# Group 0's first product in another order: M2, M1, M3, M6, M7, M5, M4 in a Winograd-tiled squared-ReLU MLP

## Chip, cores and metric

One core of one Trainium2 chip. The metric is the device time of one execution in microseconds; before the change the median of three runs is 1235.79 us (1234.95 to 1236.64).

## The reference, cut to what matters

One layer of a hybrid encoder over 1024 tokens plus 16 meta tokens, width 1024, all in float32: an input projection, stick-breaking attention, a Conformer convolution and a short gated convolution, an output projection, and then the part that the change touches:

```python
h = layer_norm(ALPHA * h + mix, ln_mix_g, ln_mix_b)
ff = jnp.square(jax.nn.relu(h @ w1)) @ w2      # w1: 1024 x 4096, w2: 4096 x 1024
h = layer_norm(ALPHA * h + ff, ln_ff_g, ln_ff_b)
return h[:, 16:]
```

## The kernel before

**Number format.** Every float32 matmul operand is split into a high part (ScalarE, L128) and a low part (VectorE, L129, the source minus the high part). A product is three passes: high x high, high x low, low x high. `split_turned` (L802) does the same with the sign turned (L807, L808).

**The MLP by groups.** The 4096 hidden columns are taken in eight groups of 512. Per group a first product (`first_product`, L915: hidden rows from h and w1, then squared ReLU) and a second product (in `group`, L1056: hidden rows times w2, added into `acc`). Both are done by Winograd's form of Strassen's scheme on 2 x 2 blocks: seven block products in place of eight, at the price of block sums and differences on VectorE. `acc` holds the normalised stream, [128 rows of a tile, 8 tiles, 1024 columns]; `order` is (6, 7, 4, 5, 0, 1, 2, 3), the order in which the output projection finishes row tiles.

**The seven operands from h.** In the first product the operands xb21, xb11 (blocks of h), xt2, xt3, xt4, xt1 (sums and differences) and xb22 are [128, 2 (high, low), 4, 512] tiles, each filled by four `x1_block` calls (L796): four transposes into one PSUM tile (tag t, three buffers; L799), then a split. For group 0 this is done while the projection ends: two x1_block calls for xb21 and xb11 per row tile (`x1_first`, L816), and for the last tiles `x1_t2` (L821): difference d3 = right half minus left half, d2 = d3 plus the other tile's left half, and the transposed, turned split into xt2. Operands that later groups use again stay in SBUF (xt1, xt2, xt4); xb21, xb11, xt3 and xb22 are written to DRAM (xscr 0 to 3, on SP's queue) and loaded again in each later group.

**Group 0 before.** M2 = early[0] x xb21 into a new pair of banks, kept as c11 (`keep_sum`, L898: two ScalarE copies). M1 = early[1] x xb11 into pair pa; c11 = relu2(c11 + pa) (`relu2`, L902: an add on VectorE, L906, ReLU and square on ScalarE, L907 and L908). Weight sums a11 += a21, part b, a11 += a22, part a; the last two x1_t2 and the blocks of xt3 (`second_half`, L1126). M6 = a x xt2 on top of pa, kept as c21. M7 = b x xt3 into pair pb, kept as c22. Then xt3 is written out and xt4 and xt1 are built (`third_half`, L1135). M4 = a22 x xt4 on top of pb, giving c21; M5 = a21 x xt1 on top of pa, giving c22; a12 += a11, xb22 is built (`last_block`, L1149), and M3 = a12 x xb22 on top of pa gives c12 straight from PSUM. `part` (L862) is a split into one of five ring buffers. The generator's yields let `group` put its own work between: the sums of the w2 blocks at the first, and at the second (before M3) the difference a21 = c22 - c21 and the splits that open the second product.

**After it.** `end_transposes` (L1158) releases the PSUM pool of the first phase, and the second product's banks come from a new pool over the same eight banks. The first matmul of the second half follows.

**What sets the order.** Program order gives each instruction its priority, and the compiler's scheduler simulates all engines and issues on each, in order, what its own model finds ready. On the chip each engine works through that fixed list. SP's queue carries the loads and stores, POOL's queue the accumulating load `w2_add` (L998).

Of the kernel before, what the change touches and what calls it, by code (L numbers as in the profile page):

```python
# [8 lines left out]
F32 = mybir.dt.float32  # L9
# [27 lines left out]
def f32(ap):  # L37
    return ap.bitcast(F32)
# [3 lines left out]
def hybrid_layer(ctx: ExitStack, tc, x, meta_tokens, ln_in_g, ln_in_b, w_in, w_conf_dw, b_conf_dw,  # L42
# [747 lines left out]
    def x_tile(pl, tag, dt=F32R):  # L790
        return pl.tile([P, 2, 4, 512], dt, tag=tag, bufs=1, name=f"x_{tag}")

    xb21, xb11, xt2 = [x_tile(x1p, tag) for tag in ("X", "Y", "T2")]
    diffs = x_tile(x1p, "T1", F32)

    def x1_block(hl, src, cols, turned=False):  # L796
        pt = ps_t([P, 4, P])
        for k in range(4):
            nc.tensor.transpose(out=pt[:, k], in_=src[:, k * P:(k + 1) * P], identity=ident)  # L799
        split_turned(hl[:, 0, :, cols], hl[:, 1, :, cols], pt, turned)  # L800
# [9 lines left out]
    def vsum(dst, a, b, op):  # L810
        nc.vector.tensor_tensor(out=dst, in0=a, in1=b, op=op)  # L811

    def cols_of(t):
        return slice(t % 4 * P, (t % 4 + 1) * P)
# [3 lines left out]
        x1_block(xb21, acc[:, t, HALF[1]], cols_of(t))  # L818
        x1_block(xb11, acc[:, t, HALF[0]], cols_of(t))

    def x1_t2(t):  # L821
        x, y = acc[:, t], acc[:, 4 + t]
        vsum(diffs[:, 0, t], x[:, HALF[1]], x[:, HALF[0]], ALU.subtract)
        vsum(diffs[:, 1, t], diffs[:, 0, t], y[:, HALF[0]], ALU.add)
        x1_block(xt2, diffs[:, 1, t], cols_of(t), True)

    done = 0
    for i in range(FIRST, 8):
        run(mix_tiles(i, i + 1))
        while done < min(4 + i - FIRST, 2 * (i - FIRST + 1)):  # L830
            if done < 4:
                x1_first(done)
            else:
                x1_t2(order[done])
            done += 1
    x = acc[:, order[7], :]
    ln_rows_dve(x, x, P, lnq[order[7]], *norm)
# [1 line left out]
        nc.sync.dma_start(out=xscr[i], in_=f32(x))  # L839
    attw.release()  # L840
    x1q = pool("x1q", side="right")
    xt4 = x_tile(x1q, "T4")

    def w1_block(k, c0):

# [16 lines left out]
    def part(src, k, turned=False):  # L862

        hl = ring("hl").rearrange("p s (k c) -> p s k c", k=k)
        split_turned(hl[:, 0], hl[:, 1], src, turned)
        return hl
# [35 lines left out]
    def relu2(r, pr, sign, more=True):  # L902

        for j, bk in pieces2(pr):
            if more:
                nc.vector.tensor_tensor(out=r[:, j], in0=bk, in1=r[:, j], op=ALU.add)  # L906
            nc.scalar.activation(out=r[:, j], in_=r[:, j] if more else bk, func=AF.Relu, scale=sign)  # L907
            nc.scalar.activation(out=r[:, j], in_=r[:, j], func=AF.Square)  # L908
# [6 lines left out]
    def first_product(g):  # L915

        r0, r1 = (wA.tile([P, 2, S], F32, tag="ff", bufs=2, name="relu2") for _ in range(2))
        c11, c12, c21, c22 = (r[:, :, h] for r in (r0, r1) for h in HALF)
        if g == 0:
            pc = pair(0)  # L920
            product1(early[0], xb21, pc, True)
            keep_sum(c11, pc)
            pa = pair(0)
            product1(early[1], xb11, pa, True)
            a11, a21, a12, a22 = w1_load(0)
            relu2(c11, pa, 1.0)
            vsum(a11, a11, a21, ALU.add)
            b = part(a11, 4)
            vsum(a11, a11, a22, ALU.add)
            a = part(a11, 4)  # L930
            xt3 = second_half()
            yield
            product1(a, xt2, pa, False)
            keep_sum(c21, pa)
            vsum(a21, a21, a22, ALU.add)
            pb = pair(0)
            product1(b, xt3, pb, True)
            keep_sum(c22, pb)
            xt1 = third_half(xt3)
            a = part(a22, 4)  # L940
            product1(a, xt4, pb, False)
            relu2(c21, pb, -1.0)
            a = part(a21, 4)
            product1(a, xt1, pa, False)
            relu2(c22, pa, -1.0)
            vsum(a12, a12, a11, ALU.add)
            x = last_block()
            xres.append(xt1)
        else:
            a11, a21, a12, a22 = w1_load(g)  # L950
            xt1 = xres[0]
            x = load_x("X", 0)
            a = part(a11, 4)
            pa = pair(g)
            product1(a, x, pa, True)
            keep_sum(c11, pa)
            vsum(a11, a11, a21, ALU.add)
            x = load_x("Y", 2)
            a = part(a11, 4)
            pb = pair(g)  # L960
            product1(a, x, pb, True)
            keep_sum(c22, pb)
            vsum(a11, a11, a22, ALU.add)
            a = part(a11, 4)
            yield
            product1(a, xt2, pa, False)
            keep_sum(c21, pa)
            a = part(a22, 4)
            product1(a, xt4, pb, False)
            relu2(c21, pb, -1.0)  # L970
            vsum(a21, a21, a22, ALU.add)
            a = part(a21, 4)
            product1(a, xt1, pa, False)
            relu2(c22, pa, -1.0)
            x = load_x("X", 1)
            a = part(a12, 4)
            pc = pair(g)
            product1(a, x, pc, True)
            relu2(c11, pc, 1.0)
            vsum(a12, a12, a11, ALU.add)  # L980
            x = load_x("Y", 3)
        a = part(a12, 4)
        yield r0, r1
        product1(a, x, pa, False)
        relu2(c12, pa, 1.0, False)
# [70 lines left out]
    def group(g):  # L1056
# [11 lines left out]
        t3, t2, t4 = b22, b12, b21  # L1068
        r0, r1 = next(steps)
        a11, a21, a12, a22 = (r[:, :, HALF[1 - th]] for r in (r1, r0) for th in range(2))  # L1070
        vsum(a21, a11, a21, ALU.subtract)
        b, a = part(b11, 2), part(a11, 2)
        w2_add(b11, g, 0, 1)
        b_, a_ = part(t3, 2), part(a21, 2)
        for _ in steps:
            pass
        if first:
            end_transposes()
        vsum(a21, a21, a22, ALU.add)
        pa = [bank2() for _ in range(2)]  # L1080
        product(a, b, pa, True)
# [41 lines left out]
        split(hl[:, 0], hl[:, 1], raw)  # L1123
        return hl

    def second_half():  # L1126

        x1_t2(order[6])
        x1_t2(order[7])
        xt3 = x_tile(x1p, "X")  # L1130
        for t in range(4):
            x1_block(xt3, diffs[:, 0, t], cols_of(t))
        return xt3

    def third_half(xt3):  # L1135

        nc.sync.dma_start(out=xscr[2], in_=f32(xt3))
        for t in range(4):
            d = diffs[:, 1, t]
            vsum(d, d, acc[:, 4 + t, HALF[1]], ALU.subtract)  # L1140
            x1_block(xt4, d, cols_of(t))
        xt1 = x_tile(x1p, "T1")
        for t in range(4):
            d = cst.tile([P, 512], F32, tag="sq", bufs=1, name="d1")
            vsum(d, acc[:, 4 + t, HALF[0]], acc[:, t, HALF[0]], ALU.subtract)
            x1_block(xt1, d, cols_of(t))
        return xt1

    def last_block():  # L1149
        xb22 = x_tile(x1p, "Y")  # L1150
        for t in range(4):
            x1_block(xb22, acc[:, t, HALF[1]], cols_of(t))
        nc.sync.dma_start(out=xscr[3], in_=f32(xb22))
        return xb22

    ps2 = None

    def end_transposes():  # L1158
# [42 lines left out]
```

## Time and profile before

| | |
|---|---|
| median of three runs | 1235.79 us |
| the profiled execution | 1235.24 us, span of the trace 1233.3 us |
| PE busy | 1151.8 us, 93% |
| DVE busy | 975.3 us, 79% |
| ACT busy | 561.8 us, 46% |
| POOL busy | 97.7 us, 8% |
| mean granted TensorE clock | 0.973 of full speed |

Times in the trace are microseconds from the start of the span. A row of a timeline gives start, length, engine, line, operation and tiles; in square brackets stands the idle time before it and what ended that. Names lose their numbers and can be those of an earlier tile in the same memory: `d3` and `d2` appear as x_T, w1's blocks as w_raw, c11 to c22 as relu. Matmuls overlap, so the length of a row holds the tail of its last one.

### The profile page before, as it was taken

How to read it: one execution, taken by the hardware profiler on the slowest of the kernel's cores; microseconds unless marked ns; L12 is line 12 of the kernel's file. 1: busy time of each engine (PE TensorE's matmuls, PEld its weight loads, DVE VectorE, ACT ScalarE, POOL GpSimd, SP SyncE). 2: the span in 40 equal slices, each digit the busy share in tenths (PEclk: the TensorE clock that was granted, in tenths of full speed). 3: DMA queues.
4: the chain of work that ended last, by engine and by line, in shares of the span. 5: the costliest groups of instructions: out<-in, count | busy, mean ns of one | idle time of the engine just before them, and what ended most of it. 6: DMA issues, size and time to landing. Idle time of an engine off the chain costs nothing.

```text
span 1233.3 us, 15574 instructions
## 1 busy us (share of the span) xinstructions
PE 1151.8 (93%) x5982; PEld 990.3 (80%) x5982; DVE 975.3 (79%) x1203; ACT 561.8 (46%) x951; POOL 97.7 (8%) x219
## 2 busy tenths in 40 slices
PE   5999997889989798998989999999999999999994
PEld 5999996779889677886768888888888888888883
DVE  6799976978878789968968688596885958859588
ACT  4522114656657556434553353433535345352444
POOL 3300002010010000034000000000000000000003
PEclk9999998899999899998999999999999999999998
DMA  9304211020021442112773653736537265372427
GB/s 293 129 20 101 69 52 51 18 52 19 18 52 35 117 141 69 53 34 85 251 258 140 221 205 108 270 116 222 209 122 278 90 222 222 134 273 72 154 69 204
DMA packets 63753, 161.80 MB, mean 131 GB/s; under 512 B 3337, under 2 KB 27184, under 8 KB 59584
## 3 DMA queue, kind: packets, MB, share of 16 engines
q1 hardware_dynamic: 56704, 144.52, 32.8%
q0 software_dynamic: 5056, 10.49, 4.6%
q10 hardware_dynamic: 1920, 5.81, 1.2%
q8 instruction: 47, 0.77, 0.3%
q14 instruction: 26, 0.21, 0.0%
HBM read 135.63 MB, written 18.87 MB: 125 GB/s over the span
## 4 chain that ended last, share of the span: by engine, by line
PE 66%; DVE 9%; ACT 4%; issue 2%; POOL 1%; DMA 1%; DVEq 0%; ACTq 0%
PE ps_g L885 24%; PE ps_g L894 24%; PE ps_g L210 6%; PE ps_g L630 5%; DVE keepp L463 2%; PE ps_t L513 2%; PE ps_g L455 2%; PE ps_o L486 1%; PE ps_o L489 1%; DVE beta L465 1%; DVE al L129 1%; ACT keepp L459 1%; DMA q_hl<-q_hl 1%; DVE acc L122 1%; ACT ah L128 0%
## 5 line engine op out<-in xcount | busy, mean ns | idle before, releaser
L894 PE MATMUL ps_g<-hl 128*128 128x512 f32 x1344 | 307.4, 390 | 2.9 <-DVE hl L129 1.6
L894 PEld LDWEIGHTS ps_g<-hl 128*128 128x128 f32 x1344 | 251.8, 188 | 57.4 <-DVE hl L129 2.0
L210 PE MATMUL ps_g<-xh,w_hl 128*128 128x346 f32 (+4 forms) x1024 | 259.8, 333 | 0.9 <-ACT beta L460 0.9
L210 PEld LDWEIGHTS ps_g<-xh,w_hl 128*128 128x128 f32 x1024 | 180.6, 192 | 10.0 <-ACT beta L460 1.1
L210 PE MATMUL ps_g<-xl,w_hl 128*128 128x346 f32 (+4 forms) x512 | 170.3, 333 | 0.7 <-DVE xl L129 0.7
L1010 DVE TENSOR_TENSOR acc<-acc,ps_g 128x1024 f32<-128x1024 f32 x96 | 116.0, 1215 | 23.2 <-PE ps_g L894 23.2
L885 PE MATMUL ps_g<-x_T,hl 128*128 128x512 f32 x576 | 133.4, 390 | 0.8 <-DVE hl L129 0.4
L885 PEld LDWEIGHTS ps_g<-x_T,hl 128*128 128x128 f32 x576 | 107.6, 188 | 24.3 <-DVE hl L129 0.8
L210 PEld LDWEIGHTS ps_g<-xl,w_hl 128*128 128x128 f32 x512 | 98.5, 192 | 5.0 <-DVE xl L129 1.0
L128 ACT CAST hl<-relu 128x1024 fp32r<-128x1024 f32 x48 | 50.6, 1054 | 106.6 <-PE ps_g L894 106.3
L463 DVE TENSOR_TENSOR_SCAN keepp<-keepp 128x912 f32<-128x912 f32 (+7 forms) x64 | 87.7, 1380 | 10.2 <-ACT keepp L459 9.6
L885 PE MATMUL ps_g<-x_Y,hl 128*128 128x512 f32 x384 | 90.5, 390 | 2.0 <-ACT x_Y L128 1.2
L885 PEld LDWEIGHTS ps_g<-x_Y,hl 128*128 128x128 f32 x384 | 71.8, 188 | 17.8 <-ACT x_Y L128 1.5
L885 PE MATMUL ps_g<-x_X,hl 128*128 128x512 f32 x360 | 84.3, 389 | 1.3 <-DVE x_X L129 1.3
L128 ACT CAST hl<-w_raw 128x1024 fp32r<-128x1024 f32 x55 | 55.4, 1049 | 62.5 <-DVE w_raw L811 62.5
L285 DVE SCALAR_TENSOR_TENSOR cacc<-glu,prm,cacc 128x482 f32<-128x482 f32 (+3 forms) x120 | 82.7, 745 | 0.3
L129 DVE TENSOR_TENSOR hl<-w_raw,hl 128x1024 fp32r<-128x1024 f32 x55 | 65.2, 1220 | 20.5 <-ACT hl L128 20.5
L885 PEld LDWEIGHTS ps_g<-x_X,hl 128*128 128x128 f32 x360 | 67.5, 188 | 15.5 <-DVE x_X L129 1.6
L906 DVE TENSOR_TENSOR relu<-ps_g,relu 128x1024 f32<-128x1024 f32 (+1 forms) x27 | 29.8, 1104 | 51.4 <-PE ps_g L885 51.4
L630 PE MATMUL ps_g<-w_hl,y 128*128 128x512 f32 x240 | 65.2, 409 | 1.8 <-DVE w_hl L129 1.7
L459 ACT ACTIVATE keepp<-ps_g 128x456 f32<-128x456 f32 (+8 forms) x112 | 51.8, 467 | 32.7 <-PE ps_g L455 14.9
L455 PE MATMUL ps_g<-ks,q_hl 128*128 128x456 f32 (+8 forms) x224 | 58.1, 362 | 8.3 <-ACT beta L460 3.9
(209 smaller groups left out, 1752.5 us busy)
## 6 DMA issues: line engine op xcount, KB each, us to landing
x_X<-xscr SPq DMA_DIRECT2D x14, 2048.0 KB, 7.7
x_Y<-xscr SPq DMA_DIRECT2D x14, 2048.0 KB, 8.4
w_raw<-in_w_ff_dram SPq DMA_DIRECT2D x16, 1024.0 KB, 8.8
w<-in_w_ff_dram SPq DMA_DIRECT2D x32, 512.0 KB, 6.5
raw<-in_w_in_dram SPq DMA_DIRECT2D x22, 512.0 KB, 4.2
b<-in_w_ff_dram SPq DMA_DIRECT2D x16, 512.0 KB, 3.6
xt<-in_x_dram SPq DMA_DIRECT2D x8, 512.0 KB, 5.2
h_scr<-ht ACTq DMA_DIRECT2D x8, 512.0 KB, 3.2
```

The source lines that it names most:

```text
L128: nc.scalar.copy(out=h, in_=src)
L129: nc.vector.tensor_tensor(out=l, in0=src, in1=f32(h), op=ALU.subtract)
L210: nc.tensor.matmul(dst[:, :cw], lhsT=w[:, a, k, :], rhs=b[:, k, c0:c0 + cw], start=(i == 0), stop=(i == 3 * KT - 1))
L285: nc.vector.scalar_tensor_tensor(out=acc, in0=glu[j][:, o + k:o + k + n], scalar=prm[:, j, k:k + 1], in1=acc, op0=ALU.mult, op1=ALU.add)
L455: nc.tensor.matmul(zp[:, :cm], lhsT=qs[h][:, m, i * P:(i + 1) * P], rhs=ks[:, h, c0:c0 + cm], start=(m == 0), stop=(m == 1 and not last))
L459: nc.scalar.activation(out=kp[h][:, c0:c0 + cw], in_=zp[:, :cw], func=AF.Sigmoid, scale=-0.125)
L463: nc.vector.tensor_tensor_scan(out=rev, data0=rev, data1=rev, initial=1.0, op0=ALU.mult, op1=ALU.bypass)
L630: nc.tensor.matmul(dst, lhsT=y[a][:, t * P:(t + 1) * P], rhs=w[b][:, n * 512:(n + 1) * 512], start=(i == 0), stop=(i == last))
L885: nc.tensor.matmul(bk, lhsT=a[:, u, k, j * P:(j + 1) * P], rhs=x[:, v, k, :], start=(start and i == 0), stop=(i == 11), skip_group_check=True)
L894: nc.tensor.matmul(prs[tt // 2][:, tt % 2], lhsT=a[:, x, u, tt * P:(tt + 1) * P], rhs=b[:, y, u, :], start=(start and i == 0), stop=(i == ...
L906: nc.vector.tensor_tensor(out=r[:, j], in0=bk, in1=r[:, j], op=ALU.add)
L1010: nc.vector.tensor_tensor(out=a, in0=a, in1=prs[h], op=op)
```

## The change

In group 0 alone the seven products come in another order: M2, M1, M3, M6, M7, M5, M4 (before: M2, M1, M6, M7, M4, M5, M3). xb22 gets a buffer of its own at once (tag Y; xb11 moves to tag T4), and the blocks of xb22 take the places that x1_t2 had among the last projection tiles. M3 goes into a pair of banks of its own and is kept as c12. The differences d3 and d2 live in two ring buffers and are made after M3, d3 being used again for xt1's differences and d2 for xt4's. M5's sum in pa then serves c22 and c12, both with an add. The last product is M4, giving c21. In `group` the splits of b11 and c22 come before the last product of group 0, and the difference a21 = c22 - c21 behind it. Later groups change only in which of xt1 and xt4 comes by `xres`.

```diff
-    xb21, xb11, xt2 = [x_tile(x1p, tag) for tag in ("X", "Y", "T2")]
-    diffs = x_tile(x1p, "T1", F32)
+    xb21, xb11, xt2, xb22 = [x_tile(x1p, tag) for tag in ("X", "T4", "T2", "Y")]
...
-    def x1_t2(t):
+    def x1_b22(t):
+        x1_block(xb22, acc[:, t, HALF[1]], cols_of(t))
+
+    def x1_t2(t, d3, d2):
         x, y = acc[:, t], acc[:, 4 + t]
-        vsum(diffs[:, 0, t], x[:, HALF[1]], x[:, HALF[0]], ALU.subtract)
-        vsum(diffs[:, 1, t], diffs[:, 0, t], y[:, HALF[0]], ALU.add)
-        x1_block(xt2, diffs[:, 1, t], cols_of(t), True)
+        vsum(d3, x[:, HALF[1]], x[:, HALF[0]], ALU.subtract)
+        vsum(d2, d3, y[:, HALF[0]], ALU.add)
+        x1_block(xt2, d2, cols_of(t), True)
...
-                x1_t2(order[done])
+                x1_b22(order[done])
...
-    xt4 = x_tile(x1q, "T4")
+    xt1 = x_tile(x1q, "T1")
...
             product1(early[1], xb11, pa, True)
             a11, a21, a12, a22 = w1_load(0)
             relu2(c11, pa, 1.0)
+            for t in order[6:]:
+                x1_b22(t)
             vsum(a11, a11, a21, ALU.add)
             b = part(a11, 4)
             vsum(a11, a11, a22, ALU.add)
+            vsum(a12, a12, a11, ALU.add)
+            a = part(a12, 4)
+            pb = pair(0)
+            product1(a, xb22, pb, True)
+            keep_sum(c12, pb)
+            d3, d2 = (f32(ring("diffs")).rearrange("p s (t c) -> p (s t) c", t=2) for _ in range(2))
+            for t in order[4:]:
+                x1_t2(t, d3[:, t], d2[:, t])
             a = part(a11, 4)
-            xt3 = second_half()
-            yield
             product1(a, xt2, pa, False)
             keep_sum(c21, pa)
-            vsum(a21, a21, a22, ALU.add)
+            nc.sync.dma_start(out=xscr[3], in_=f32(xb22))
+            xt3 = x_tile(x1p, "X")
+            for t in range(4):
+                x1_block(xt3, d3[:, t], cols_of(t))
             pb = pair(0)
             product1(b, xt3, pb, True)
             keep_sum(c22, pb)
-            xt1 = third_half(xt3)
+            nc.sync.dma_start(out=xscr[2], in_=f32(xt3))
+            yield
+            vsum(a21, a21, a22, ALU.add)
+            for t in range(4):
+                vsum(d3[:, t], acc[:, 4 + t, HALF[0]], acc[:, t, HALF[0]], ALU.subtract)
+                x1_block(xt1, d3[:, t], cols_of(t))
+            a = part(a21, 4)
+            product1(a, xt1, pa, False)
+            for r, sign in ((c22, -1.0), (c12, 1.0)):
+                relu2(r, pa, sign)
+            xt4 = x_tile(x1p, "T4")
+            for t in range(4):
+                vsum(d2[:, t], d2[:, t], acc[:, 4 + t, HALF[1]], ALU.subtract)
+                x1_block(xt4, d2[:, t], cols_of(t))
+            xres.append(xt4)
             a = part(a22, 4)
+            yield r0, r1
             product1(a, xt4, pb, False)
             relu2(c21, pb, -1.0)
-            a = part(a21, 4)
-            product1(a, xt1, pa, False)
-            relu2(c22, pa, -1.0)
-            vsum(a12, a12, a11, ALU.add)
-            x = last_block()
-            xres.append(xt1)
+            return
...
-        vsum(a21, a11, a21, ALU.subtract)
         b, a = part(b11, 2), part(a11, 2)
         w2_add(b11, g, 0, 1)
+        if first:
+            run(steps)
+            end_transposes()
+        vsum(a21, a11, a21, ALU.subtract)
         b_, a_ = part(t3, 2), part(a21, 2)
-        for _ in steps:
-            pass
-        if first:
-            end_transposes()
+        run(steps)
```

`second_half`, `third_half` and `last_block` are removed; what they did stands in the lines above.

## Rows read from the trace of the kernel before

**Rows 1.** The page's busy time, share of the span and instructions, by engine.

```profile
PE   1151.8 (93%) x5982; PEld 990.3 (80%) x5982; DVE 975.3 (79%) x1203; ACT 561.8 (46%) x951; POOL 97.7 (8%) x219
```

**Rows 2.** The chain that ended last: start, us, what.

```profile
643.75 38.37 PE ps_g L894 x168
...
1177.16 27.21 PE ps_g L894 x120
```

**Rows 3.** Windows: us, busy time by engine (instructions), PE clock, DMA share, GB/s.

```profile
573.60:616.00 42.40, 33.49 (x151) 25.80 (x150) 40.87 (x54) 23.01 (x40) 5.11 (x11) 0.84 0.63 225
616.00:643.75 27.75, 24.43 (x121) 18.68 (x119) 16.89 (x23) 15.33 (x26) 0.28 (x1) 1.00 0.72 259
...
587.70:643.75 56.05, 50.29 (x241) 39.39 (x239) 43.65 (x56) 31.47 (x51) 1.28 (x1) 0.97 0.75 263
643.75:1210.00 566.25, 564.65 (x2489) 467.08 (x2490) 427.39 (x385) 241.67 (x243) 10.97 (x12) 1.00 0.48 172
...
580.00:585.00 5.00, 3.47 (x13) 2.12 (x11) 5.00 (x6) 2.25 (x5) 1.16 (x3) 0.50 0.00 0
585.00:590.00 5.00, 4.18 (x14) 3.31 (x15) 5.00 (x8) 1.19 (x2) 0.00 (x0) 0.50 0.50 210
590.00:595.00 5.00, 5.00 (x24) 4.13 (x23) 3.58 (x7) 1.99 (x3) 0.00 (x0) 0.90 0.99 418
```

**Rows 4.** Timeline of PE, 587 to 645 us: M2 and the rows with waits.

```profile
587.71 6.81 PE L885 MATMUL ps_g<-x_X,w_slot 128*128 128x512 f32 x22
...
597.47 4.83 PE L885 MATMUL ps_g<-x_Y,hl 128*128 128x512 f32 x20 [0.72 <-DVE hl L129]
...
605.00 4.83 PE L885 MATMUL ps_g<-x_T,hl 128*128 128x512 f32 x20 [0.41 <-DVE hl L129]
...
612.47 5.29 PE L885 MATMUL ps_g<-x_X,hl 128*128 128x512 f32 x22 [1.31 <-DVE x_X L129]
...
619.42 0.73 PE L885 MATMUL ps_g<-x_T,hl 128*128 128x512 f32 x2 [0.34 <-ACT x_T L128]
...
627.52 0.66 PE L799 MATMUL ps_t<-ident,d 128*128 128x128 f32 x4 [0.94 <-DVE d L811]
...
637.04 6.02 PE L885 MATMUL ps_g<-x_Y,hl 128*128 128x512 f32 x24 [1.24 <-ACT x_Y L128]
643.75 26.59 PE L894 MATMUL ps_g<-hl 128*128 128x512 f32 x116 [0.69 <-ACT relu L907]
```

**Rows 5.** Timeline of DVE, 573 to 587 us, in front of M2.

```profile
573.67 0.69 DVE L811 TENSOR_TENSOR x_T<-acc 128x512 f32<-128x512 f32 x1
574.27 0.68 DVE L129 TENSOR_TENSOR x_X<-ps_t,x_X 128x512 fp32r<-128x512 f32 x1
...
585.06 1.22 DVE L811 TENSOR_TENSOR w_raw<-w_raw 128x1024 f32<-128x1024 f32 x1
586.20 0.69 DVE L129 TENSOR_TENSOR x_X<-ps_t,x_X 128x512 fp32r<-128x512 f32 x1
```

**Rows 6.** Timeline of ACT at the end of M2.

```profile
592.03 0.59 ACT L900 COPY relu<-ps_g 128x512 f32<-128x512 f32 x1 [3.34 <-PE ps_g L885]
592.51 1.05 ACT L128 CAST hl<-w_raw 128x1024 fp32r<-128x1024 f32 x1
```

**Rows 7.** Timelines of DVE and ACT at the end of the first half.

```profile
634.96 0.69 DVE L906 TENSOR_TENSOR relu<-ps_g,relu 128x512 f32<-128x512 f32 x1 [1.81 <-PE ps_g L885]
...
636.88 0.64 ACT L908 ACTIVATE relu<-relu 128x512 f32<-128x512 f32 x1
...
637.63 1.21 DVE L811 TENSOR_TENSOR relu<-relu 128x1024 f32<-128x1024 f32 x1
...
641.03 1.22 DVE L129 TENSOR_TENSOR hl<-relu,hl 128x1024 fp32r<-128x1024 f32 x1
```

**Rows 8.** Timeline of SP's queue: group 1's load of x_Y.

```profile
644.71 0.32 SPq L912 DMA_DIRECT2D x_Y<-xscr  x1
```

**Rows 9.** DMA issues, 560 to 650 us: engine, count, KB each, us to landing.

```profile
b<-in_w_ff_dram POOLq DMA_DIRECT2D x1, 512.0 KB, 11.4
```

More of the change, by code (lines that the diff above doesn't have):

```diff
@@ L938, in first_product @@
             keep_sum(c22, pb)
-            xt1 = third_half(xt3)
+            nc.sync.dma_start(out=xscr[2], in_=f32(xt3))
[13 more added lines that the diff above has]
+            xres.append(xt4)
             a = part(a22, 4)
+            yield r0, r1
             product1(a, xt4, pb, False)
             relu2(c21, pb, -1.0)
-            a = part(a21, 4)
-            product1(a, xt1, pa, False)
-            relu2(c22, pa, -1.0)
-            vsum(a12, a12, a11, ALU.add)
-            x = last_block()
-            xres.append(xt1)
+            return
         else:
             a11, a21, a12, a22 = w1_load(g)
-            xt1 = xres[0]
+            xt4 = xres[0]
             x = load_x("X", 0)
@@ L1124, in early_part @@
         return hl
[L1126 to L1154, printed above, removed]
     ps2 = None
```

## The prediction

> **What bounds the kernel now.** I read the busy shares first, then the chain that ended last, then the windows, then the timelines of single engines. The busy shares put PE at 93% and DVE at 79% of the span [rows 1]: an average that says where the room is not. The chain places it: from 643.75 us on it is unbroken PE work, one 38 us piece per half group, to the last group [rows 2], and the windows say the same (564.65 us busy of 566.25) [rows 3]. So whatever brings forward the first matmul of group 0's second half, at 643.75, brings the whole rest forward by as much; nothing later can swallow it, and nothing later can give more.
>
> The stretch before, from the last projection matmul at 573.60 to 643.75, is where PE waits. It falls in two. Up to 616.0 DVE is busy 40.87 of 42.40 us; from there to 643.75 only 16.89 of 27.75 [rows 3]. The front is DVE's, the rear is PE's with holes. From the start of M2's main run at 587.71, PE is busy 50.29 of 56.05 us [rows 3]. The holes have names in PE's timeline: 0.72 at M1 (its weights' low half), 0.41 at M6 (the same), 1.31 at M7 (a block of x_X), 0.34 at M4 (a block of x_T), 0.94 at a transpose (a difference d), 1.24 at M3 (a block of x_Y), and 0.69 at the very end, where the second half waits for the last read of the first half's PSUM [rows 4]. The first six sum to 4.96 us.
>
> **The change, part by part.** The seven products, the 28 blocks of transposes and the sixteen half-row differences all stay; their order changes.
>
> *Two more adds and copies.* M3 becomes a product of its own, so c12 is kept (two ScalarE copies, 0.59 each [rows 6]) and added later (two DVE adds of 0.69 [rows 7]); its two ReLUs read SBUF instead of PSUM. On DVE, half-row operations start 0.60 apart and full ones 1.14 [rows 5]; two adds cost 1.2 us of DVE's time. They follow M5, while PE runs M4; in the rear DVE has 10.9 us free [rows 3]. On the path: 0. If DVE were full there, 1.2.
>
> *Start of M2.* DVE runs without a gap from 573.60 to M2 and the last x_X low half goes at 586.20 [rows 5]. In front of it stand four differences for T2 (573.67 is one); they move behind M3 and release 4 x 0.60 = 2.4 us. In their place come at most two low halves of B22 blocks, 1.2 us, which may also go after M2's operand. A weight sum at 585.06 stands in front of the last x_X too [rows 5]; if it is the one for M5, moved behind M7 in the code, it may give another 1.14. Ends: 0 (the gaps are filled by other ready work) and 3.6 us. I take **1.8 us**, half the sum of the ends and between 1.2 and 2.4, what the counted operations give by themselves.
>
> The granted clock was 0.50 from 580 to 590, after PE had idled, and came back during 590 to 595, where PE was busy the whole 5 us (mean 0.90) [rows 3]; M2's 22 matmuls took 6.81 us against 5.29 for the 22 of M7 [rows 4], a loss of 1.5 us. I let this loss move with M2 unchanged. The Trainium skill (TensorE: Matmul & The Clock Gate, Part 1 on the clock gate) says that it is PE's own activity that lifts the throttle, not time since some event. By that, the loss stays 1.5 us and the sum below holds; were the return fixed at about 591 us, M2 starting 1.8 us earlier would win about 0.9 us less.
>
> *The six holes.* Before, M6 follows M1 in the same bank and M4 follows M7 in the same bank, each behind a read of that bank. Now every product that accumulates has another between: M3 between M1 and M6, M5 between M7 and M4. B22's blocks need only finished rows, so M3's 1.24 us wait on x_Y has no cause left. Does DVE deliver each operand in time? From M2 at 585.9 (1.8 us earlier), with 5.5 us a product, 0.5 a block (38.37 us for 168 matmuls [rows 2]; the blocks are my estimate from the 0.66 us that one block takes alone in the 627.52 row [rows 4], less overlap):
> - M3 is due at 585.9 + 6.8 + 1 + 5.5 = 599.2. DVE owes before it the last rows' norm, an x_Y half, four B22 halves, M1's low half, three weight sums and two low halves: 7 x 1.14 + 5 x 0.60 = 11, so 596.9.
> - M6 is due at 599.2 + 5.5 + 2 = 606.7. DVE owes two adds, eight differences, four T2 halves, one low half: 14 x 0.60 + 1.14 = 9.5, so 606.4. This is the tight one.
> - M7: 2.4 us of DVE, ready at 608.8, due at 614.2.
> - M5: three W2 sums, one weight sum, one low half and eight half operations, 10.5, so 619.3 against 621.7.
> - M4: 4.8 + 1.14 + 1.14 (b11's low half), so 626.4 against 629.2.
>
> PE's due times are strict here: by them M4 would end at 634.7, 3 us before what the old timeline gives once 1.8 and 3.5 us are taken off (638.4 for the second half's start), since they hold no cost of switching between transposes and products.
>
> The order on DVE and ScalarE is fixed by a scheduler's own estimate, not by these due times (M1's cast stands behind c11's copy, which waits 3.34 us, on ScalarE [rows 6]), so some of the holes will reappear: I let 1.5 of the 4.96 come back. Gain **3.5 us**; ends 0 and 5.0.
>
> *The end.* What ends the first half changes from c12 to c21, and c21 feeds the second product of the second half. Chain behind M4's last matmul: add 0.69, ReLU and square 0.64 each, difference 1.21, cast 1.05, low half 1.22 [rows 6, 7], 5.4 us plus hand-overs, some 5.8. Its cover is the first product of the second half (c22 and b11, both ready), which starts about 0.7 after M4, as before, and lasts 5.5: 6.2. Hidden by 0.4 if nothing stands before it on DVE. The next sum on a21, another full operation, and the cast and low half for the third product also slip behind M4. I charge **0.5 us**; ends 0 and 2.5 (two full DVE operations in the way).
>
> *DMAs and queues.* On SP, xscr[3] is written before xscr[2] instead of 25 us after it, and both before M5; group 1's loads of x_X and x_Y wait for these writes and for M7 and M3, all earlier now (x_Y's load went at 644.71 [rows 8], needed by 682). Group 1's W1 loads wait for the parts of a21 and a22, which move later by about 10 us, but are needed only after 38 us of PE work. POOL's accumulating load of b11 (11.4 us to land [rows 9]) is next read some 22 us after the second half begins. Cost 0; if that cover went, group 1 would open with a hole of a few us. Ring buffers: the two differences take two of five, and each later part finds one freed by a finished product: 0.
>
> **Sum:** 1.8 + 3.5 - 0.5 = 4.8 us less. The profiled execution took 1235.24, 0.55 below the median of 1235.79; off the median that is **1231.0 us**. The ends: 3.6 + 5.0 = 8.6 less, 1227.2; and 2.5 more, 1238.3.
>
> **Rivals.** 0.2%, 2.5 us, is about what a measurement of this kernel can tell from no change.
> - *DVE takes the holes back.* For it: up to 616 DVE is nearly full, M6 is met within 0.3 us above, and the change adds 1.2 us to DVE. Then waits at M1, M3, M6 and M5 replace the old ones, M2 gains 1.2 and the holes about 0.5: 1.7 - 0.5 = 1.2 less, 1234.6. Against: 10.9 us of idle DVE behind 616 that moved work can use. Chance 0.22, a fifth of it still faster than 1233.3.
> - *The order does not take.* The scheduler may issue M3 late or the differences early all the same, as it now runs differences ahead of x_X halves [rows 5]. About 1235. Chance 0.06, since each engine still has to serve M3 first in the code.
> - *Slower: c21's chain lies open.* If the first product of the second half is held as well (c22's part queued behind the adds on DVE), or stands behind c21's part, PE idles through the whole 5.8 us and the two or three full operations behind it for the third product, some 8 us in all. It decides once the wait at the second half's opening passes 5.3 + 2.5 = 7.8 us. Time: 1235.8 - 5.3 + 8 = 1238.5. For it: that add, two activations, a difference and a split all follow the last product, where before only a ReLU did. Both DVE and ScalarE serve their queues strictly in order, as the Trainium skill says too (TensorE: Matmul & The Clock Gate, "Architectural detail", on queue depths), and ScalarE's 3.34 us wait in front of a ready cast [rows 6] agrees. Against: c22 is finished one product ahead. Chance 0.10.
>
> **How the numbers follow.** The forecast (gain of 2.5 to 8.6 us) has 0.62; with the fifth of the first rival, faster is 0.66; the rest of it and the second make 0.24 for the same; slower is 0.10. A range from 1227.0 to 1236.5 leaves out the slower rival and a little of the far ends.
>
> **What would show it.** In the changed trace: M3 as third product with no wait on x_Y; M2's main run near 586; holes between M2 and M4 of 1 to 2 us in sum instead of 4.96; the wait in front of the second half still about 0.7, and its second product's wait under 1; that half's start near 638.4; unbroken PE after it. It is wrong if M2 has not moved (the DVE term), if waits on hl or on differences of 4 us or more stand before M6 and M5 (the holes), or if the first two products of the second half wait several us on a part of relu (the end).

## The result, and the profile after

The changed kernel takes 1242.72 us (median of 6 runs, 1240.89 to 1244.47) against 1235.86 for the kernel before on the same chip (6 runs, 1234.95 to 1236.64): ratio 1.0061, 95% interval 1.0049 to 1.0073, 6.9 us slower. The prediction was 1231.0, in the range 1227.0 to 1236.5. The profiled execution took 1242.26 us, span 1240.3, mean clock 0.972. One execution below, of run 8's ten, took 1458.1 us at a mean clock of 0.748 and is left out of that run's ratio.

The page's busy shares hardly differ from [rows 1]: DVE has the 1.1 us that two more adds cost, PE 3.8 us more for the same 5982 matmuls.

```profile
PE 1155.6 (93%) x5982; PEld 993.4 (80%) x5982; DVE 976.4 (79%) x1205; ACT 563.4 (45%) x953; POOL 96.6 (8%) x219
```

So the difference is in waiting and in slow PE time, and the timeline of PE places it. Its columns: start, duration, engine, line, operation, tiles, shape, count, and in brackets the idle time in front and what ended it.

```profile
584.47 1.97 PE L798 MATMUL ps_t<-ident,acc 128*128 128x128 f32 x8 [0.52 <-DVE x_T L129]
586.09 5.71 PE L887 MATMUL ps_g<-x_X,w_slot 128*128 128x512 f32 x22
...
592.43 5.73 PE L887 MATMUL ps_g<-x_T,hl 128*128 128x512 f32 x24
599.87 1.20 PE L887 MATMUL ps_g<-x_Y,hl 128*128 128x512 f32 x4 [1.71 <-ACT hl L128]
602.88 6.45 PE L887 MATMUL ps_g<-x_Y,hl 128*128 128x512 f32 x20 [1.81 <-DVE hl L129]
609.18 1.47 PE L798 MATMUL ps_t<-ident,diffs 128*128 128x128 f32 x12
613.60 2.44 PE L798 MATMUL ps_t<-ident,diffs 128*128 128x128 f32 x12 [2.95 <-DVE x_T L807]
615.68 6.70 PE L887 MATMUL ps_g<-x_T,hl 128*128 128x512 f32 x24
...
624.98 0.73 PE L887 MATMUL ps_g<-x_X,hl 128*128 128x512 f32 x2 [1.29 <-ACT x_X L128]
...
643.35 6.01 PE L887 MATMUL ps_g<-x_T,hl 128*128 128x512 f32 x24 [1.24 <-ACT x_T L128]
650.23 12.05 PE L896 MATMUL ps_g<-hl 128*128 128x512 f32 x52 [0.88 <-DVE relu L908]
662.52 2.83 PE L896 MATMUL ps_g<-hl 128*128 128x512 f32 x11 [0.24 <-ACT hl L128]
```

M2 and M1 are ahead of the kernel before: M2's main run starts at 586.09 against 587.71 (0.4 us of it because the projection ended earlier in this execution), and M1 is done at 598.2 against 602.3. Then M3, the new third product, waits twice for its weights (hl), 3.52 us together, and runs slowly (6.45 us for 20 matmuls; 20 of M1 took 4.83 in [rows 4]). M6 waits 2.95 us for its operand and is slow too. M7, M5 and M4 each wait 1.24 to 1.29 us for the cast of a block of their operand. The second half opens at 650.23 against 643.75, 6.5 us later; behind it PE is as unbroken as before, with one more hole of 0.24 us.

The account of the 6.5 us, from these rows and those of before: waits from M2 on 11.64 us against 5.65 (+6.0); M2 1.6 earlier and 1.1 shorter (-2.7); M3 slower by 1.6 and M6 with its transposes by 1.9 (6.70 against 5.73 for M1's 24 here, 2.44 against 1.47 for 12 transposes): +6.8 in sum, 0.3 more than measured.

What held up M3 and M6 stands in the timelines of DVE and ACT.

```profile
590.91 1.23 DVE L129 TENSOR_TENSOR hl<-w_raw,hl 128x1024 fp32r<-128x1024 f32 x1 [2.91 <-ACT hl L128]
593.40 1.23 DVE L129 TENSOR_TENSOR hl<-w_raw,hl 128x1024 fp32r<-128x1024 f32 x1 [1.27 <-ACT hl L128]
...
599.21 2.48 DVE L810 TENSOR_TENSOR diffs<-acc 128x512 f32<-128x512 f32 x4
601.62 1.22 DVE L129 TENSOR_TENSOR hl<-w_raw,hl 128x1024 fp32r<-128x1024 f32 x1
...
607.43 1.22 DVE L810 TENSOR_TENSOR w<-w,b 128x1024 f32<-128x1024 f32 x1
...
609.82 1.89 DVE L810 TENSOR_TENSOR diffs<-diffs,acc 128x512 f32<-128x512 f32 x3
611.63 1.22 DVE L129 TENSOR_TENSOR hl<-w_raw,hl 128x1024 fp32r<-128x1024 f32 x1
612.76 1.88 DVE L807 SCALAR_TENSOR_TENSOR x_T<-ps_t,x_T 128x512 fp32r<-128x512 f32 x3
...
615.16 0.68 DVE L807 SCALAR_TENSOR_TENSOR x_T<-ps_t,x_T 128x512 fp32r<-128x512 f32 x1
```

```profile
591.84 0.59 ACT L902 COPY relu<-ps_g 128x512 f32<-128x512 f32 x1 [0.96 <-PE ps_g L887]
592.32 1.05 ACT L128 CAST hl<-w_raw 128x1024 fp32r<-128x1024 f32 x1
```

Two things. First, the cast of b, M7's weights, stands on ACT behind the second copy of c11, which waits for M2, and that of M1's weights in the same way behind the first. DVE is idle for 2.91 + 1.27 us meanwhile, and M3's weights, two sums behind b, start from 593.40. Second, where DVE does work, other ready work stands ahead of what PE needs next: four differences for T2 (2.48 us) ahead of M3's low half at 601.62, which M3 gets at 602.84; then the three sums of W2 (607.43 is one), the differences for M4 (609.82) and M5's low half at 611.63, 6.5 us together, ahead of M6's low halves, which begin at 612.76 and end at 615.84.

The slow stretches are the granted clock, here the windows around M3's second hole (columns: window, its length, PE, PEld, DVE, ACT and POOL busy, PE clock, DMA share, GB/s).

```profile
601.00:602.00 1.00, 0.07 (x1) 0.00 (x0) 1.00 (x3) 0.82 (x2) 0.00 (x0) 1.00 1.11 461
602.00:603.00 1.00, 0.12 (x1) 0.12 (x2) 1.00 (x2) 0.00 (x0) 0.00 (x0) 1.00 1.14 483
...
605.00:606.00 1.00, 1.00 (x4) 0.76 (x3) 1.00 (x3) 0.00 (x0) 0.00 (x0) 0.50 0.69 295
606.00:607.00 1.00, 1.00 (x4) 0.81 (x3) 1.00 (x2) 0.44 (x1) 0.00 (x0) 0.50 0.08 33
...
608.00:609.00 1.00, 1.00 (x6) 0.80 (x5) 0.97 (x2) 0.00 (x0) 0.00 (x0) 1.00 0.00 0
```

PE idled in 601 to 603 at full grant; the grant went to 0.50, the lower of its two levels (1.2 GHz), only when PE was busy again, from 604 to about 607.5. So M3 paid for its hole a second time, 1.6 us.

### The profile page after: what moved, and what is told of

The parts are those of the page before. It is cut to its first block, busy times and chain, and to the rows that moved or that the text cites. A ratio compares the mean times of both kernels' runs of the same rounds, so it can differ in the third digit from the quotient of the medians.

```text
span 1240.3 us, 15578 instructions
## 1 busy us (share of the span) xinstructions
PE 1155.6 (93%) x5982; PEld 993.4 (80%) x5982; DVE 976.4 (79%) x1205; ACT 563.4 (45%) x953; POOL 96.6 (8%) x219
## 4 chain that ended last, share of the span: by engine, by line
PE 65%; DVE 10%; ACT 4%; issue 2%; POOL 1%; DMA 1%; DVEq 0%; ACTq 0%
PE ps_g L896 24%; PE ps_g L887 24%; PE ps_g L210 6%; PE ps_g L630 5%; DVE keepp L463 2%; PE ps_t L513 2%; PE ps_g L455 2%; PE ps_o L486 1%; PE ps_o L489 1%; DVE beta L465 1%; DVE al L129 1%; ACT keepp L459 1%; DVE diffs L810 1%; DVE hl L129 1%; DMA q_hl<-q_hl 1%
## 5 line engine op out<-in xcount | busy, mean ns | idle before, releaser
L887 PE MATMUL ps_g<-x_T,hl 128*128 128x512 f32 x600 | 139.8, 392 | 2.5 <-ACT x_T L128 2.5
L887 PEld LDWEIGHTS ps_g<-x_T,hl 128*128 128x128 f32 x600 | 113.0, 189 | 26.9 <-ACT x_T L128 3.0
L887 PE MATMUL ps_g<-x_Y,hl 128*128 128x512 f32 x360 | 86.1, 395 | 3.5 <-DVE hl L129 1.8
L887 PEld LDWEIGHTS ps_g<-x_Y,hl 128*128 128x128 f32 x360 | 68.6, 191 | 18.8 <-DVE hl L129 2.2
```

The source lines that it names most:

```text
L887: nc.tensor.matmul(bk, lhsT=a[:, u, k, j * P:(j + 1) * P], rhs=x[:, v, k, :], start=(start and i == 0), stop=(i == 11), skip_group_check=True)
```

## The experiments

Two theories. **Placing**: the order of the products is sound; what costs is where the scheduler's fixed order puts each cast, sum and split on ACT and DVE, ahead of what the next product needs. **Chain**: in the new order every product needs its own blocks turned, cast and split right in front of it, and this takes longer than a product, whatever stands in the queues. The first four expectations have narrower names: 'gate' (the late ring) and 'fillers' (work pulled forward) are two forms of placing, 'order' is the chain. In the edits, `issue_after(x)` queues what is built under it behind the instruction x on the same engine; `lows` collects the low halves of the operands' blocks. As the projection's end differs by up to 3.6 us between profiled executions, the length of the **stretch** is given beside the time: from the end of the projection's last matmul to the second half's first. It is 69.75 us before (574.00 to 643.75) and 76.63 after (573.60 to 650.23). Each time stands against the runs of the kernel before on the same chip.

**1. The fillers alone.** The sums of W2, M5's sum and split and M4's differences go behind M6's last low half.

```diff
+            t2_low = lows[-1].ins
...
+            with tc.issue_after(t2_low):
+                vsum(a21, a21, a22, ALU.add)
...
+            with tc.issue_after(t2_low):
+                a = part(a21, 4)
...
+                with tc.issue_after(t2_low):
+                    vsum(d2[:, t], d2[:, t], acc[:, 4 + t, HALF[1]], ALU.subtract)
...
+        with tc.issue_after(low) if first else ExitStack():
+            vsum(b22, b22, b12, ALU.add)
+            vsum(b12, b22, b11, ALU.add)
+            vsum(b21, b12, b21, ALU.add)
```

> The changed kernel with one thing added: on DVE the three W2 sums, the sum for M5's weights, their low half and the four differences for xt4 are queued behind the last low half of xt2. Theory 'fillers' (DVE is full from 593.4 to 618.2 and some 7 us of it is work that the scheduler pulled forward while M6 waits): M6's wait of 2.95 us and the cold clock behind it go, 3 to 5 us less than the changed kernel's 1242.7, so 1238 to 1240; M3's wait of 3.5 us stays. Theory 'gate' (M3's weights come late because the ring buffers are given out only after M2): under 1.5 us less, since M6 then waits for its transposes behind a late M3. Theory 'order' (a third product on fresh operands can't be fed, whatever the placing): no change, the waits only move to M7.

Measured: 1243.36 us, ratio 1.0072 (1.0055 to 1.0089). PE's timeline at M7:

```profile
624.65 1.09 PE L800 MATMUL ps_t<-ident,diffs 128*128 128x128 f32 x4 [3.19 <-DVE x_X L129]
625.39 7.45 PE L888 MATMUL ps_g<-x_X,hl 128*128 128x512 f32 x22
```

M6's 2.95 us is down to 0.59 (and 0.32 a little later), and M7 waits 3.19 us instead and runs slowly: the same work, now ahead of the next operand. The 1238 to 1240 expected of 'fillers' did not come; both theories allow this outcome.

**2 and 3. The ring free earlier, in the new and in the old order.** The ring of `part` takes over the memory that held the first weights, those of M2. The edit puts them elsewhere; run 3 does the same to the kernel before. In run 2 the casts of M1's and b's weights start at 576.50 and 582.39; in the changed kernel they stand behind c11's copies, at 589.82 and 592.32.

```diff
-    early = [attq.tile([P, 9, 2, 2, 64], F32R, tag="v", bufs=2, name="w_slot")[:, :8].rearrange(
-        "p (s k) b c d -> p s k (b c d)", s=2)]
+    early = [big(wA, "ff", 2, "w_first").rearrange("p s (k c) -> p s k c", k=4)]
```

> The changed kernel with M2's weights in a buffer of the pool wA (tag ff) instead of the attention pool, so that the ring buffers no longer wait for M2 to end. Theory 'gate': the casts of M1's and b's weights move from behind c11's copies (589.8 and 592.3 us) to before 582, the chain to M3's weights ends before M1 does, M3's two waits (1.71 and 1.81 us) and the 1.6 us of slow clock in it go: 4 to 5 us less, 1237.5 to 1239. Theory 'fillers': M3 gains, but M6 then waits longer for DVE by the same amount: 0 to 1.5 us less, 1241 to 1242.7. Theory 'order': as fillers.

> Control: the kernel before (old order of products) with the same move of M2's weights into wA. Theory 'gate' says that the late ring costs the old order little, as it waited only 0.72 us at M1 and 0.41 at M6 for low halves: 0.5 to 1.5 us less than 1235.9. If the old order gains 4 us or more too, the gate is no property of the new order, and the comparison of orders has to be made with the ring free in both.

Measured: 1241.53 us, ratio 1.0055 (1.0040 to 1.0070), and for the old order 1241.60, ratio 1.0057 (1.0043 to 1.0072), stretches of 74.86 and 76.42. Both expectations of 'gate' failed, a gain of 4 to 5 us in the new order and of 0.5 to 1.5 in the old. In the new order M3's two waits fall from 3.52 to 2.08 us, but M2 is later. In the old order PE's timeline shows, at M6, where [rows 4] had a wait of 0.41, now 0.67 and:

```profile
609.06 2.29 PE L799 MATMUL ps_t<-ident,x_T 128*128 128x128 f32 x8 [1.92 <-DVE x_T L808]
611.00 6.67 PE L885 MATMUL ps_g<-x_T,hl 128*128 128x512 f32 x19
```

This is the run that speaks most plainly: the kernel before, its order untouched, loses 7 us to one buffer that comes free earlier, as much as the change cost. DVE's timeline of it shows why M2 is late already:

```profile
586.74 1.22 DVE L811 TENSOR_TENSOR w_raw<-w_raw 128x1024 f32<-128x1024 f32 x1
587.88 1.22 DVE L811 TENSOR_TENSOR w<-w,w 128x1024 f32<-128x1024 f32 x1
589.01 1.22 DVE L129 TENSOR_TENSOR hl<-w_raw,hl 128x1024 fp32r<-128x1024 f32 x1
590.15 0.68 DVE L129 TENSOR_TENSOR x_X<-ps_t,x_X 128x512 fp32r<-128x512 f32 x1
```

A weight sum, a sum of W2 and a weights' low half, 3.4 us, stand ahead of the last low half that M2 waits for. The weight sum stood there before too [rows 5]; the other two are new, and so is M1's low half, at 580.28. M2's main run starts 16.6 us after the projection's end, against 13.7. The late ring had been holding early work back.

**4 and 5. Ring and lead, with and without the fillers queued.** The lead: T2's differences and blocks are built ahead of M3's matmuls, so that PE turns them before M3 and not behind it.

```diff
+            d3, d2 = (f32(ring("diffs")).rearrange("p s (t c) -> p (s t) c", t=2) for _ in range(2))
+            for t in order[4:]:
+                x1_t2(t, d3[:, t], d2[:, t])
             pb = pair(0)
             product1(a, xb22, pb, True)
             keep_sum(c12, pb)
-            d3, d2 = (f32(ring("diffs")).rearrange("p s (t c) -> p (s t) c", t=2) for _ in range(2))
-            for t in order[4:]:
-                x1_t2(t, d3[:, t], d2[:, t])
```

> The changed order with all three: M2's weights in wA, xt2's differences and blocks written ahead of M3's product in the program (so that PE turns them before or during M3), and DVE's early work queued behind xt2's last low half. Theories 'gate' and 'fillers' together: M3's 3.5, M6's 2.95 and about 2.3 us of slow clock go, 1242.7 - 8 = about 1234, below the kernel before. Theory 'order': still over 1236, with a wait of 3 us or more in front of M3, M6 or M7.

> The changed kernel with the free ring and T2's blocks ahead, nothing queued on VectorE: what the two give without the placing. Theory 'placing decides': early sums, differences and splits still stand ahead of M6's and M7's low halves, waits of 2 us or more remain there: 1238.5 to 1242. Rival 'ring and lead alone are the cure': 1232 to 1235.

Measured: with the fillers queued 1238.51 us, ratio 1.0028 (1.0018 to 1.0037), stretch 72.95; without 1238.98, ratio 1.0035 (1.0021 to 1.0049), stretch 74.70. Run 4 was expected at about 1234 by 'gate' and 'fillers', so it counts for 'order'; run 5 came out as placing had it, but its waits stand elsewhere than expected. M6 now follows M3 without a wait in both. What is left with the fillers queued is M7, in PE's timeline:

```profile
618.35 1.09 PE L800 MATMUL ps_t<-ident,diffs 128*128 128x128 f32 x4 [3.41 <-DVE x_X L129]
619.09 7.04 PE L888 MATMUL ps_g<-x_X,hl 128*128 128x512 f32 x22
```

and without, M2 (1.68 us for x_X) and M3 (1.24 and 2.44 for x_Y, then 6.46 us for 18 matmuls). Ring and lead are no cure by themselves.

**6, 7 and 8. Everything queued behind whole operands; the old order with the same care.** M5's work goes behind M7's last low half, M4's and the sums of W2 behind M5's last; run 6 without the ring, run 7 with it, both with the lead. Run 8 is the kernel before with the sums of W2 and the later weights' sums and splits behind M7's last low half.

```diff
+            x3_low = lows[-1].ins
...
+            with tc.issue_after(x3_low):
+                vsum(a21, a21, a22, ALU.add)
...
+            x1_low = lows[-1].ins
...
+                with tc.issue_after(x1_low):
+                    vsum(d2[:, t], d2[:, t], acc[:, 4 + t, HALF[1]], ALU.subtract)
```

> The changed kernel with two edits and the late ring kept: T2's differences and blocks turned ahead of M3's matmuls, and on VectorE M5's sums, differences and weights queued behind M7's operand, and the sums of W2, M4's differences and weights queued behind M5's operand. Theory 'the next product's operand stands behind other ready work': M6's wait (2.95 us) and its slow stretch (about 0.7) go, no later product gets a wait over 1.4 us, and what is left is M3's (1.71 + 1.81 us and about 1.6 of slow clock), whose chain starts behind the copies of c11 on ScalarE: 1242.7 - 4 = about 1238.5 (1237 to 1240). Rival 'each block needs turning, cast and low half, and these take longer than a product': the wait reappears in M7, M5 or M4 at 2.5 to 4 us as it did when only the fillers were queued behind M6, and the time is 1242 to 1244.

> The same two edits and the free ring (first weights in another buffer), which starts M3's chain early. Theory 'other work stands ahead of the operand': against the run with ring, lead and fillers (1238.5, M7 waits 3.41 us and runs about 1.7 us slow) M7's wait falls to under 0.7 and its slow stretch goes: about 1234 (1232 to 1235.5), the span from the projection's last matmul to the second half's first at 68 to 70 us against 73.35 there and 70.15 in the kernel before. Rival 'the chain of a block is longer than a product': a wait of 2.5 us or more stands in M5 or M4 in place of M7's, and the time stays 1237.5 to 1239.5.

> Control: the kernel before, its order of products and its ring kept, with the sums of W2 and the weights' sums and splits of M4, M5 and M3 queued on VectorE behind M7's operand, the same care as in the other two. If the queueing helps any order (its gain in the two others then says nothing against the new order): one wait of 1.3 us and some of the others' 0.3 to 0.9 go, 1233 to 1234.5. If it is the new order alone that is hurt by work placed ahead of operands: 1235 to 1237, no change.

Measured: 1242.55 us, ratio 1.0068 (1.0052 to 1.0083), stretch 76.87; with the ring 1240.98, ratio 1.0057 (1.0039 to 1.0076), stretch 72.80; the old order 1234.25, ratio 0.9994 (0.9984 to 1.0004), stretch 68.36. My expectation failed for the first two: M7's wait shrank to 0.78 and stood at M5 and M4 again, as the chain theory had it, and run 7 took even longer than the 1237.5 to 1239.5 that it allowed. In the old order queueing made no difference that is clear of the spread: the waits at M6 and M7 went, but one of 1.67 us for a difference stands in front of M4, which then takes 6.90 us for 22 matmuls. Run 7, PE's timeline, then DVE's:

```profile
626.24 0.66 PE L800 MATMUL ps_t<-ident,diffs 128*128 128x128 f32 x4 [2.17 <-DVE x_T L129]
...
638.24 0.66 PE L800 MATMUL ps_t<-ident,diffs 128*128 128x128 f32 x4 [3.30 <-DVE x_T L129]
```

```profile
609.75 1.29 DVE L129 TENSOR_TENSOR x_X<-ps_t,x_X 128x512 fp32r<-128x512 f32 x2 [0.48 <-ACT x_X L128]
616.11 1.29 DVE L129 TENSOR_TENSOR x_X<-ps_t,x_X 128x512 fp32r<-128x512 f32 x2 [5.07 <-ACT x_X L128]
617.32 1.22 DVE L811 TENSOR_TENSOR w_raw<-w_raw 128x1024 f32<-128x1024 f32 x1
```

But DVE's rows tell the two theories apart: between the second and the third low half of x_X it was idle for 5.07 us, since PE turned the last two blocks only behind M6's matmuls, and everything queued behind the last low half sat that out.

**9 and 10. Placed between the pairs.** The same edit, with the marks two low halves earlier, and the sums of W2 behind M5's last; run 9 with ring and lead, run 10 with the lead alone.

```diff
-            x3_low = lows[-1].ins
+            x3_low = lows[-3].ins
...
-            x1_low = lows[-1].ins
+            x1_low, x1_last = lows[-3].ins, lows[-1].ins
```

> As the run with the free ring, T2's blocks ahead and queueing, but the queueing placed one pair of blocks earlier: M5's sum, differences and weights behind the second of M7's four low halves (VectorE was idle for 5.07 us between the second and the third there), M4's differences and weights behind the second of M5's, the sums of W2 behind M5's last. Theory 'where VectorE's static order puts each piece of work decides, and the order of the products does not': M5's waits (2.17 + 0.68 us) and M4's (3.30 + 1.00) fall to under 1.3 each, 1240.98 - 4.5 = about 1236.5; by the span from the projection's last matmul to the second half's first 72.80 - 4.5 = 68.3 us (67.3 to 70), below the 69.75 of the kernel before. Rival 'the new order has too little room for turning, cast and low half whatever stands on VectorE': the waits come back elsewhere and that span stays 72 to 73.5 us.

> The same placing with the late ring of the change kept, so that M3's chain starts behind the copies of c11. By the first theory only M3's waits stay (1.72 + 1.82 us there, perhaps 1 us of slow clock): 1242.55 - 6 = about 1236.5 (1235 to 1238.5), and M5 and M4 wait under 1.3 us each; by the rival 1241 to 1243.

Measured, run 9: **1232.00 us** (10 runs) against 1235.38, ratio 0.9977 (0.9963 to 0.9991), stretch 67.17. Run 10: 1239.73, ratio 1.0035 (1.0021 to 1.0048), stretch 72.93. Run 9, PE's timeline, then DVE's in what had been the idle 5 us:

```profile
586.41 5.36 PE L888 MATMUL ps_g<-x_X,w_first 128*128 128x512 f32 x22
...
598.87 0.73 PE L888 MATMUL ps_g<-x_Y,hl 128*128 128x512 f32 x2 [0.80 <-ACT x_Y L128]
...
624.25 0.73 PE L888 MATMUL ps_g<-x_T,hl 128*128 128x512 f32 x2 [1.29 <-ACT x_T L128]
...
633.06 6.14 PE L888 MATMUL ps_g<-x_T,hl 128*128 128x512 f32 x24 [1.15 <-ACT x_T L128]
640.07 12.05 PE L897 MATMUL ps_g<-hl 128*128 128x512 f32 x52 [0.88 <-DVE relu L909]
```

```profile
608.85 1.21 DVE L811 TENSOR_TENSOR w_raw<-w_raw 128x1024 f32<-128x1024 f32 x1
609.98 1.29 DVE L811 TENSOR_TENSOR diffs<-acc 128x512 f32<-128x512 f32 x2
```

The same products and the same instructions on VectorE as in run 7, in another order, and 9 us less (run 7 was 6.7 us above the kernel before on its chip, run 9 is 3.4 below): no wait over 1.29 us is left and no slow stretch behind M2. Of the 7.9 us between the two profiled executions the stretch explains 5.6; in the other 2.3 the projection ended earlier, which is not shown to be the placing's doing. So the time is well below the 1236.5 expected, the stretch only just below its 67.3 to 70. This is what placing foretold: the loss of 6.9 us is not the new order's own. What is left of the chain are waits of 0.80 to 1.29 us in front of four products. Run 10 took longer than its 1236.5: M5's and M4's waits fell to 1.28 and 1.32 and M3's 3.5 us stayed, about as expected, but M3 took 6.22 us for 19 of its matmuls and M5 6.91 for 22, against 5.30 in run 9, a slow stretch that I had not counted. The ring is needed for M3.

**11. The sums of W2 on GpSimd.** Run 9 with those three sums of group 0 taken from VectorE.

```diff
-            vsum(b22, b22, b12, ALU.add)
-            vsum(b12, b22, b11, ALU.add)
-            vsum(b21, b12, b21, ALU.add)
+            for d, u, v in ((b22, b22, b12), (b12, b22, b11), (b21, b12, b21)):
+                nc.gpsimd.tensor_tensor(out=d, in0=u, in1=v, op=ALU.add)
```

> As the first of these, with the three sums of W2 (1.22 us each on VectorE) on GpSimd for group 0, so that VectorE has 3.7 us less to do in the stretch. If VectorE's load itself still sets the end: up to 2 us below the first run. If only the order sets it: within 0.7 us of the first run. If GpSimd's sums come too late for the second half or slow VectorE down: over 1 us above it.

Measured: 1239.37 us, ratio 1.0035 (1.0023 to 1.0048), stretch 73.66, 7.4 us above run 9. The timelines of POOL and of DVE:

```profile
581.59 2.37 POOL L1098 TENSOR_TENSOR w<-w,w 128x1024 f32<-128x1024 f32 x1
584.03 3.23 POOL L1098 TENSOR_TENSOR w<-w,b 128x1024 f32<-128x1024 f32 x1
```

```profile
581.78 3.26 DVE L122 SCALAR_TENSOR_TENSOR acc<-acc,mv,norm 128x1024 f32<-128x1024 f32 x1
584.96 0.68 DVE L129 TENSOR_TENSOR x_T<-ps_t,x_T 128x512 fp32r<-128x512 f32 x1
585.56 2.79 DVE L129 TENSOR_TENSOR hl<-w_raw,hl 128x1024 fp32r<-128x1024 f32 x1
```

GpSimd did the sums as soon as it could, in front of M2, and the operations of VectorE beside them took 3.26 and 2.79 us instead of 1.28 and 1.22. Each ended 1.1 us after the sum beside it (583.96 and 585.04; 587.26 and 588.35), so each waited for that sum to end; the one between them, which reads PSUM, kept its 0.68 us. M2's main run starts 3.4 us later than in run 9, at 589.77. With 7.08 us for M2's 22 matmuls against 5.36, and 6.87 for M5's against 5.30, that is the 6.5 us by which the stretch is longer. Nothing was late for the second half; VectorE was stopped.

**12. One more piece placed.** Run 9 with the first weight sum queued behind M2's last low half.

```diff
+            with tc.issue_after(lows[6].ins):
+                vsum(a11, a11, a21, ALU.add)
-            vsum(a11, a11, a21, ALU.add)
```

> As the run with ring, lead and the placing between pairs (1232.0), with one piece more placed: the first sum of the weights (a11 plus a21), and so the split and the sums behind it, queued on VectorE behind the last low half of M2's operand. Ahead of that low half stood two such pieces (1.22 us of the sum, 1.22 us of the split). Theory 'placing decides': M2's main run starts 1.2 to 2.4 us earlier after the projection's last matmul (13.9 us there, 12.5 us in the changed kernel), M3 waits no longer, 1230 to 1231.5. Rival 'M2's start is set by the normalization of the last row tile, which has its own chain': M2 within 0.6 us of there and 1231.5 to 1232.5; or M3's chain becomes late by what M2 gained, and the time stays.

Measured: 1235.11 us (11 runs), ratio 1.0001 (0.9989 to 1.0013), stretch 68.90. M2's main run starts 12.4 us after the projection's last matmul ends instead of 13.5 (the 13.9 of the expectation counts from that matmul's start), but M3 waits 1.32 and 0.86 us where run 9 had 0.80 and 0.16: the rival's second half. What M2 gained was lost at M3, and more. Of the 3.1 us between the two medians, the stretch explains 1.7; the rest lies ahead of it or in the spread of the runs.

## Why the prediction was wrong

**Start of M2: nearly right.** 1.6 us earlier against 1.8 predicted, or 1.2 counted from the projection's end. M2's loss to the clock did not move with it, as I had put it; it shrank from 1.5 us to 0.4, 5.71 us for 22 matmuls against 6.81, a gain that the sum did not have. The grant was back within 585 to 590, with a mean of 0.80 where [rows 3] has 0.50:

```profile
585.00:590.00 5.00, 5.00 (x22) 4.32 (x21) 3.00 (x5) 1.83 (x4) 0.00 (x0) 0.80 0.87 357
```

So a return fixed at about 591, the other case of the prediction, is ruled out. PE was busy from 584.47 on without a gap, where before it waited 0.62 us just ahead of M2. That agrees with the Trainium skill (TensorE: Matmul & The Clock Gate, Part 1 on the clock gate), by which PE's own activity lifts the throttle.

**The end: right.** 0.88 us in front of the second half against 0.69, and 0.24 us at its second product: 0.4 against 0.5 predicted. The rival that c21's chain would lie open did not come true. The DMAs cost nothing, and the two adds nothing on the path.

**The six holes: wrong, and here the prediction failed.** It had M3's operands ready at 596.9 for 599.2 and M6's at 606.4 for 606.7, let 1.5 of 4.96 us of holes come back, and bounded the term below by 0. Measured: 10.76 us of holes. The step that failed is the table of due times itself. It added up what DVE owes before each product, as if DVE served it in that order and without a pause. M3's last low half came at 602.84, 5.9 us after my 596.9. DVE waited 4.2 us for casts behind c11's copies, and T2's differences and c11's adds, 3.6 us, which it owed only to M6, went first; a weight sum and most of a norm, 2.1 us of what I had counted, were done before M2: 5.7 in sum. M6's last low half came at 615.84, 9.4 us after my 606.4: those 5.9, less the 3.6 already done, and 7.1 of W2's sums, M4's differences and M5's low half, owed only later. I had the row for the first (the cast behind c11's copy [rows 6]) and cited it, but put no price on it; nor is that cast shown to have been ready there, for it starts at 575.88 once its buffer is free (run 3). The floor of 0 was wrong because a change of order changes what every engine finds ready, not only what the moved product needs; run 3 shows that the same happens to the old order when one buffer comes free sooner.

**The rival that came nearest** was "DVE takes the holes back", at 1234.6. Its mechanism is what happened at M6, but it could at most undo the gain. It had neither M3's weights behind ScalarE nor the clock: M3 and M6 lost about 3.5 us to slow stretches behind their holes.

**What the expectation of 1231 was worth.** Run 9, with the new order, ring, lead and the placing that the due times silently assumed, takes 1232.0. That it lies near 1231 is luck. M2's main run starts only 0.2 us earlier after the projection's end than before, and the holes behind it sum to 4.84 us, hardly fewer than before: what it gains is PE's busy time from M2's main run to the second half, 47.82 us against 50.28, with 1.45 of M2's slow clock in it, and not the holes that I had counted on. How much of run 9's 0.23% is the order's own stays open, since the old order with its later work queued has 0.9994 and the intervals of the two overlap between 0.9984 and 0.9991. The old order with ring, lead and placing together was not tried.

## What to carry to other kernels

Where two engines are each busy for some three quarters of a stretch, a sum of what an engine owes before a deadline says only that an order exists, not that the kernel has it: read in the timeline which ready work the fixed order puts ahead of each operand, and price that. A buffer that comes free late may be what holds such work back, so freeing it can cost as much as a bad order; and queueing work behind the last piece of an operand can be as bad as leaving it ahead, if the engine idles in the middle of the operand. A hole in PE may have to be paid twice, for itself and for a slow clock behind it, and the second price is not fixed, as the next section shows.

## What the hardware showed that was not expected

- The granted clock fell after the hole, not in it: full in 601 to 603 with PE nearly idle, then 0.50 in 605 to 607 with PE busy the whole time, at a cost of 1.6 us to M3's 20 matmuls.
- The price of a hole varies. Behind the same two waits in front of M5, 2.17 and 0.68 us, its 24 matmuls took 8.61 us in run 6 and 6.05 in run 7 (the granted clock was 0.50 from 630 to 636 in run 6 and 1.00 for the whole of M5 in run 7); behind waits of 1.28 and 0.15 us its 22 took 6.91 in run 10 and, behind 1.29 and 0.15, 5.30 in run 9. What decides this is not shown.

```profile
630.05 8.61 PE L888 MATMUL ps_g<-x_T,hl 128*128 128x512 f32 x24 [0.68 <-ACT x_T L128]
627.57 6.05 PE L888 MATMUL ps_g<-x_T,hl 128*128 128x512 f32 x24 [0.68 <-ACT x_T L128]
```

- Sums of 128 x 1024 float32 on GpSimd took 2.37 to 3.23 us each, against 1.22 on VectorE, and an operation of VectorE with both inputs in SBUF did not run beside one but after it (3.26 and 2.79 us from start to end). The Trainium skill says so (SBUF — State Buffer, "Who interferes with whom"): such an instruction contends with one of GpSimd that reads SBUF, and the pair of ports that they share is an exclusive lock. These rows agree. I had it only as the third outcome of run 11. Taking 3.7 us of work off VectorE in this way made the kernel 7.4 us slower.
